# Mixing stage in another program order, weights requested two ahead, state chain on VectorE; FFN 2 with six classical tiles

## Chip, cores and metric

One core of a Trainium2 chip runs the whole layer. The metric is the device time of one execution in microseconds (us); several executions are taken and the median counts. Engines: TensorE (PE; its weight loads are PEld), VectorE (DVE), ScalarE (ACT), GpSimd (POOL) and SyncE (SP), which here issues nearly all DMAs.

## What is computed

One decoder layer on a sequence of 512 tokens with 1024 channels: a half-step SwiGLU FFN, a mixing stage in which half of the channels go through a diagonal state space model (SSM, 32 groups of 16 channels, a complex state of 64 each) and half through sliding-window attention (8 heads, 2 key/value heads, window 128, sinks, partial rotary), a second half-step FFN, and a last RMSNorm. In short:

```python
h = rms_norm(x, ffn1_norm);  x = x + 0.5 * swiglu(h, w_gate, w_up, w_down)
h = rms_norm(x, mix_norm) @ w_in          # u (512), q (512), k (128), v (128)
y_ssm = s5_mixer(u)                       # B u -> scan over time -> C -> gelu -> y * sigmoid(y @ w_glu + b)
y_att = swa_sink_attention(rope(q), rope(k), v, sinks)
x = x + concat(rms_norm(y_ssm), rms_norm(y_att)) @ w_out
h = rms_norm(x, ffn2_norm);  x = x + 0.5 * swiglu(h, w_gate2, w_up2, w_down2)
return rms_norm(x, final_norm)
```

All of it is float32, with an FFN width of 2816, that is 22 tiles of 128 (called f).

## The kernel before

**Products.** A float32 operand is split into a rounded part hi and a rest lo, and a product is three matmuls (`mm3`, L178 to L184: hi with hi, lo with hi, hi with lo). A weight is fetched by `weight` (L173): a DMA of 512 KB on SyncE's queue into `wraw` (L169), a rounding copy `whi` (ACT unless the table ENGINES names another engine, L152) and the subtraction `wlo` (VectorE by default, L171). Each of the three tiles has three buffers (pool `wp`), so a fourth request waits until the first weight's subtraction has read its `wraw`. SyncE issues in program order: a DMA that waits for its buffer holds back all behind it.

**Stages.** FFN 1 runs to about 400 us of the span, the mixing stage from there to some 591, FFN 2 to the end. The Tile scheduler orders each engine's instructions from the program order by its own simulation; pools decide which buffer is free when.

**Mixing.** The program order is written out in the string ORDER (L43); each word is a step with an index: U0 to U3 project u by a 128x512 weight each (`u_mm`, 24 matmuls of 512 columns), K0 and K1 project k and v (48 matmuls of 256 columns each), C0 to C3 project q (`tok_mm`, L1011 to L1013, tiles pt). R0 and R1 make the norm's factors; u0 to u3 scale by them and store u to a DRAM buffer `du` (L1100, L1102); l0 and l1 load half of it back as U in another layout (L1108, eight DMAs each), after the stores have landed. P0 and P1 (`ssm_state`) do the state of one half each: 32 + 32 matmuls pv with matV (L1131), four products ri (L1136 to L1139), sums zr and zi, two scans wr and wi (L1144, L1145), four products ro (L1148) and eight pieces S (L1160). L0 (`load_matT`, L966) loads matT, 2 MB, by eight DMAs of 256 KB whose rows are 512 bytes; it comes to lie in a buffer (tag "big", two of them) that one half of matV has, so it waits for P1's matmuls. Y0 and Y1 (`ssm_out`) are the matmuls with matT and U (L1175) and with matC and S (L1176). k, t, q, Q, S, E, T, V are the attention's steps; G is the SSM's gate (weight wglu), W and X the output projection (weight wout). The string ENGINES (L47) gives single instructions another engine: G is GpSimd, V VectorE, A ScalarE. By default the ro products alternate between VectorE and GpSimd, and zr and zi are GpSimd's.

**FFN 2** (`ffn2`). The first NCL tiles f are classical: 2 x 24 matmuls of 512 columns each for gate and up. The others come in pairs of tiles, and each pair is done by a seven-product (Strassen-Winograd) scheme on quarters, 2 x 7 x 4 x 3 = 168 matmuls of 256 columns (`pairs`, L513). The quarters of the normed input and their sums have to be made and split first (`quarters`, eight steps: h at L440, splits xq at L459 and L462, sums on GpSimd). PREP says how many of these steps are placed behind tile f; the rest follow one by one in the first down product. FGROUPS[2] cuts the f tiles into groups; after each group but the last `down` multiplies by the group's part of w_down, eight outputs of 128 channels (dn), and adds to x. The last group is the tail.

```python
def weight(self, src, cols, key=""):
    t = self.weight_tiles()
    self.weight_part(t, src, 0, cols, key)
    return t[1][:, :cols], t[2][:, :cols]
```

Of the kernel before, what the change touches and what calls it, by code (L numbers as in the profile page):

```python
# [29 lines left out]
HD = 64  # L30
HALF = 8
EPS = 1e-6
FGROUPS = {1: ((0, 6), (6, 12), (12, 17), (17, 22)), 2: ((0, 4), (4, 10), (10, 14), (14, 18), (18, 22))}
HEADS = [0, 1, 4, 5, 2, 3, 6, 7]
TAIL_EARLY = 0
PR_AT = (0, 0, 1)
PRB_AT = (0, 1, 3)
NCL = 4
AHEAD = 2
PREP = (1, 1, 0)  # L40
SCALED = -1.0 / 8192.0
RND = 12582912.0
ORDER = ("R0 K0 U1 K1 U0 R1 u0 U2 U3 u1 k0 l0 C0 u2 u3 P0 l1 t0 C1 P1 C2 L0 C3 q0 q3 Y0 q2 q1 Q2 Y1 Z0 Q0 Q1 "  # L43
# [3 lines left out]
ENGINES = ("higlu1=G hiout00=G loglu1=G loout00=G lowq3=G pt01=V pt11=V pt20=A pt21=V pt30=A pt31=V pt41=V "  # L47
         "pt51=V ql1=G ql3=G ro00=G ro02=G ro10=G ro11=V rope83=G s0000=G s0001=G s0010=G s0100=G s0101=G "
         "s1011=G s1111=G y001=A y011=A yh000=V yh100=V yh101=V yh111=V yl000=G yl010=G yl110=G zi0=V zr0=V "
         "zr1=V")  # L50
PIO2 = [float.fromhex("0x1.92p+0"), float.fromhex("0x1.fb4p-12"), float.fromhex("0x1.4442d18469899p-24")]


def lay_out(inp):
# [17 lines left out]
    out["wgs2"] = c(pr.transpose(0, 2, 1, 3, 4, 5).reshape((NF - NCL) // 2, 2, 2, P, 8 * P))  # L72
    f0 = FGROUPS[2][-1][0]
    out["wdt"] = c(g["ffn2_w_down"][0, f0 * P:].reshape(NF - f0, P, D))
# [58 lines left out]
class Body:  # L133
# [231 lines left out]
    def ffn(self, i, next_gain, extra):  # L365
# [7 lines left out]

        groups = FGROUPS[i]
        hooks = {(1, 1): self.first_norm, (2, 1): self.norm_bcast}
# [209 lines left out]
    def ffn2(self):  # L585
        xg, wgu, wd = self.xg, self.d["wgu2"], self.d["wd2"]
        prep, acts, pend = [], [], []
        for gi, (f0, f1) in enumerate(FGROUPS[2]):
            acts = []
            f = f0  # L590
            while f < f1:
# [22 lines left out]
                f += 1  # L614
            if gi == len(FGROUPS[2]) - 1:
                self.tail_weights(1)
# [351 lines left out]
    def mixing(self):  # L968
        nc, d = self.nc, self.d
        V, A, G, PE = nc.vector, nc.scalar, nc.gpsimd, nc.tensor  # L970
# [16 lines left out]
        self.y = [None] * 4  # L987
        self.ys = [None] * 4

        def u_mm(m):  # L990
            wh, wl = self.weight(d["wu"][m].rearrange("p k m -> p (k m)"), 1024, f"u{m}")
            pu[m] = self.ps("pu")
            for k in range(KT):
                self.mm3(pu[m], wh[:, k * P:(k + 1) * P], wl[:, k * P:(k + 1) * P], xg[k][0], xg[k][1],
                         k == 0, k == KT - 1)
# [4 lines left out]
        def tok_mm(wname, c, n, nk):  # L1000
            key = (wname, c)
            if c == 0:
                hold[wname] = [self.ps("pt") for _ in range(4)]
            wh, wl = self.weight(d[wname][c].rearrange("p k m -> p (k m)"), 1024, f"{wname}{c}")
            for kk in range(nk):
                k = c * nk + kk
                for t in range(4):
                    xs = [xg[k][i][:, t * P:(t + 1) * P] for i in range(2)]
                    wsl = slice(kk * n, (kk + 1) * n)
                    o = hold[wname][t][:, 0:n]  # L1010
                    PE.matmul(o, xs[0], wh[:, wsl], start=(k == 0), stop=False)  # L1011
                    PE.matmul(o, xs[0], wl[:, wsl], start=False, stop=False)
                    PE.matmul(o, xs[1], wh[:, wsl], start=False, stop=(k == KT - 1))  # L1013
# [49 lines left out]
        wt, po = {}, {}  # L1063

        def out_half(half, m):
            key = (half, m // 2)
            if key not in wt:
                wt[key] = self.weight(d["wout"][half, m // 2].rearrange("p k m -> p (k m)"), 1024, f"out{half}{m // 2}")
            w = wt[key]
            ps = po[half, m] = self.ps("ow")  # L1070
            for k in range(4):
                c = ((m % 2) * 4 + k) * P
                src = (self.s2, self.attn)[half][k]
                self.mm3(ps, w[0][:, c:c + P], w[1][:, c:c + P], src[0], src[1], k == 0, k == 3)
# [130 lines left out]
    def glu(self, m):  # L1205
        nc = self.nc
        if m % 2 == 0:
            self.wg = self.weight(self.d["wglu"][m // 2].rearrange("p k m -> p (k m)"), 1024, f"glu{m // 2}")
        ps = self.ps("glu")
        for k in range(4):  # L1210
            c = ((m % 2) * 4 + k) * P
            self.mm3(ps, self.wg[0][:, c:c + P], self.wg[1][:, c:c + P], self.ys[k][0], self.ys[k][1], k == 0, k == 3)
        sg = self.m2(name="sg")
        nc.scalar.activation(sg, ps, AF.Sigmoid, bias=self.b_glu[:, m:m + 1])
        y2 = self.m2(name="y2")
        self.eng(f"y2{m}").tensor_tensor(y2.rearrange("p (n s) -> p s n", s=T), self.y[m].rearrange("p (s n) -> p s n", s=T),
                                sg.rearrange("p (s n) -> p s n", s=T), op=ALU.mult)
        self.ss_ssm.add(y2, last=(m == 3))
        self.y2.append(y2)
# [294 lines left out]
```

## Time and profile before

| | us |
|---|---|
| three runs | 969.84, 961.62, 962.42 |
| median | 962.42 |
| profiled execution | 968.99 |
| its span, first to last instruction | 967.2 |
| PE busy in it | 921.6 (95%) |
| DVE busy | 649.9 (67%) |
| ACT busy | 377.2 (39%) |
| POOL busy | 348.1 (36%) |

The span is 1.8 us shorter than the execution's own time; times of single instructions are counted from the span's start. The profiled execution had a mean granted TensorE clock of 0.971. Busy shares are means over three stages: the rows below are taken from the places that the change touches.

### The profile page before, as it was taken

The numbers are of one execution on the slowest core, as the hardware profiler recorded it, in microseconds if no ns is written. First come the engines' busy times: TensorE is split into PE (matmuls) and PEld (weight loads), VectorE is DVE, ScalarE is ACT, GpSimd is POOL, SyncE is SP. The second block draws the span as 40 slices with busy tenths as digits, with TensorE's granted clock in tenths as the row PEclk, the third lists the DMA queues.
The fourth block names the chain that finished last, engine by engine and source line by source line (L and its number), as shares of the span: only waits on it lengthen the run. The fifth ranks groups of instructions, "written<-read, shape, count | busy, mean of one in ns | idle before, by whom it ended". The sixth has DMA issues, their size and how long they took to land.

```text
span 967.2 us, 13609 instructions
## 1 busy us (share of the span) xinstructions
PE 921.6 (95%) x5108; PEld 787.4 (81%) x5108; DVE 649.9 (67%) x1171; ACT 377.2 (39%) x685; POOL 348.1 (36%) x305
## 2 busy tenths in 40 slices
PE   9899899999999999999399999979999999999996
PEld 6687688888887888888388887858998898998995
DVE  7984445555644444756797478698985585886876
ACT  7132122222232223422197334434553353453553
POOL 3109411459910000405631045084550540724602
PEclk9899999999999999999798799989999999999998
DMA  6321423343323322435901032214413403405322
GB/s 234 109 83 50 119 87 121 56 134 114 93 63 118 113 70 66 145 111 151 120 1 45 1 100 74 77 43 143 139 43 111 156 23 101 140 23 170 105 65 88
DMA packets 47313, 91.95 MB, mean 95 GB/s; under 512 B 13200, under 2 KB 19088, under 8 KB 47248
## 3 DMA queue, kind: packets, MB, share of 16 engines
q1 hardware_dynamic: 46816, 90.54, 31.7%
q8 instruction: 40, 0.66, 0.3%
q10 hardware_dynamic: 432, 0.55, 0.2%
q14 instruction: 25, 0.20, 0.1%
HBM read 87.44 MB, written 3.64 MB: 94 GB/s over the span
## 4 chain that ended last, share of the span: by engine, by line
PE 77%; DVE 11%; POOL 4%; issue 3%; ACT 3%; DMA 1%; SPq 0%; DVEq 0%; POOLq 0%; ACTq 0%
PE gu L180 9%; PE gu L182 9%; PE gu L181 9%; PE dn L182 7%; PE dn L180 7%; PE dn L181 7%; PE gua L182 3%; PE gua L180 3%; PE gua L181 3%; POOL tB L632 3%; DVE wlo L534 2%; PE guc L182 2%; PE ow L180 2%; PE ow L181 2%; PE ow L182 2%
## 5 line engine op out<-in xcount | busy, mean ns | idle before, releaser
L152 ACT CAST whi<-wraw 128x1024 fp32r<-128x1024 f32 (+5 forms) x138 | 119.3, 875 | 317.1 <-PE gu L181 120.7
L171 DVE TENSOR_TENSOR wlo<-wraw,whi 128x1024 fp32r<-128x1024 f32 (+5 forms) x137 | 152.7, 1121 | 36.5 <-ACT whi L152 36.2
L182 PE MATMUL gu<-hi,wlo 128*128 128x512 f32 x416 | 164.6, 397 | 4.5 <-DVE wlo L171 4.5
L180 PE MATMUL gu<-hi,whi 128*128 128x512 f32 x416 | 167.2, 406 | 1.3 <-ACT hi L193 1.1
L181 PE MATMUL gu<-lo,whi 128*128 128x512 f32 x416 | 164.7, 397 | 0.1
L182 PE MATMUL dn<-hi,wlo 128*128 128x512 f32 (+1 forms) x336 | 130.1, 395 | 3.7 <-DVE wlo L171 3.7
L180 PE MATMUL dn<-hi,whi 128*128 128x512 f32 (+1 forms) x336 | 130.2, 396 | 2.5 <-ACT hi L201 2.4
L181 PE MATMUL dn<-lo,whi 128*128 128x512 f32 (+1 forms) x336 | 131.4, 393 | 0.0
L182 PEld LDWEIGHTS gu<-hi,wlo 128*128 128x128 f32 x416 | 78.9, 190 | 23.1 <-DVE wlo L171 4.9
L267 POOL TENSOR_TENSOR sq<-sq 128x512 f32<-128x512 f32 x24 | 35.3, 1472 | 166.2 <-ACT sq L263 163.1
L180 PEld LDWEIGHTS gu<-hi,whi 128*128 128x128 f32 x416 | 79.1, 190 | 19.7 <-ACT hi L193 1.9
L181 PEld LDWEIGHTS gu<-lo,whi 128*128 128x128 f32 x416 | 79.1, 190 | 17.7 <-DVE lo L195 1.0
L182 PEld LDWEIGHTS dn<-hi,wlo 128*128 128x128 f32 x336 | 64.2, 191 | 19.5 <-DVE wlo L171 5.0
L180 PEld LDWEIGHTS dn<-hi,whi 128*128 128x128 f32 x336 | 64.1, 191 | 18.3 <-ACT hi L201 2.9
L181 PEld LDWEIGHTS dn<-lo,whi 128*128 128x128 f32 x336 | 64.3, 191 | 13.8
L499 POOL TENSOR_TENSOR s<-s,wraw 128x512 f32<-128x512 f32 x36 | 59.5, 1653 | 39.4 <-DMA wraw<-wgs 25.7
L499 POOL TENSOR_TENSOR s<-wb 128x512 f32<-128x512 f32 x18 | 26.6, 1477 | 116.1 <-DMA wb<-wgs 108.9
L534 DVE TENSOR_TENSOR wlo<-s,whi 128x512 fp32r<-128x512 f32 x72 | 58.0, 849 | 9.0 <-ACT whi L533 9.0
L410 DVE SCALAR_TENSOR_TENSOR x<-dn,x 128x512 f32<-128x512 f32 x32 | 21.7, 687 | 47.9 <-PE dn L182 47.9
L533 ACT CAST whi<-s 128x512 fp32r<-128x512 f32 x72 | 41.4, 618 | 31.8 <-PE gua L181 9.4
L343 DVE TENSOR_TENSOR u<-gu,R 128x512 f32<-128x512 f32 x26 | 17.8, 686 | 49.7 <-PE gu L182 49.0
L426 DVE SCALAR_TENSOR_TENSOR x<-dn,x 128x512 f32<-128x512 f32 x32 | 21.7, 687 | 35.6 <-PE dn L182 35.6
(376 smaller groups left out, 2164.6 us busy)
## 6 DMA issues: line engine op xcount, KB each, us to landing
wraw<-wgu SPq DMA_DIRECT2D x50, 512.0 KB, 3.5
wraw<-wd SPq DMA_DIRECT2D x24, 384.0 KB, 3.2
wb<-wgs SPq DMA_DIRECT2D x36, 256.0 KB, 4.6
wraw<-wgs SPq DMA_DIRECT2D x18, 512.0 KB, 3.8
wraw<-wd SPq DMA_DIRECT2D x24, 256.0 KB, 2.7
wraw<-wd SPq DMA_DIRECT2D x16, 320.0 KB, 2.9
wraw<-wout SPq DMA_DIRECT2D x8, 512.0 KB, 3.5
x<-xT SPq DMA_DIRECT2D x8, 256.0 KB, 5.0
```

Source lines behind the costliest of these rows:

```text
L152: (e.copy if e is self.nc.scalar else e.tensor_copy)(out, x)
L171: self.eng("lo" + key).tensor_tensor(lo, raw, hi.bitcast(F32), op=ALU.subtract)
L180: mm(out, wh, xh, start=start, stop=False, **kw)
L181: mm(out, wh, xl, start=False, stop=False, **kw)
L182: mm(out, wl, xh, start=False, stop=stop, **kw)
L267: b.nc.gpsimd.tensor_tensor(self.acc, self.acc, sq, op=ALU.add)
L410: nc.vector.scalar_tensor_tensor(self.x[m], ps, 0.5, self.x[m], op0=ALU.mult, op1=ALU.add)
L426: self.nc.vector.scalar_tensor_tensor(self.x[m], ps, 0.5, self.x[m], op0=ALU.mult, op1=ALU.add)
L499: add = lambda o, x, y: nc.gpsimd.tensor_tensor(o, x, y, op=ALU.add)
L533: self.chained("A", lambda: A.copy(hi[:, c], w))
L534: self.chained("V", lambda: V.tensor_tensor(lo[:, c], w, hi[:, c].bitcast(F32), op=ALU.subtract))
L632: (eng or V).tensor_tensor(out, a, b, op=op)
```

## The change

**Mixing.** ORDER has U0, U1 and U2 ahead of K0 and K1, the first load of U (l0) and P0 earlier, and the first and second half of K before and after P0. ENGINES puts all ro products and zr and zi of both halves on VectorE and names no engine for S, whose default is VectorE. `fetch` takes the place of `weight` for the stage's 16 weights: it lists them in the order in which ORDER first needs them, and a step that takes one also requests those up to WAHEAD - 1 further in the list.

**FFN 2.** NCL goes from 4 to 6, so one pair less is left; the groups are three of six tiles and the tail; PREP has five entries instead of three.

```diff
-FGROUPS = {1: ((0, 6), (6, 12), (12, 17), (17, 22)), 2: ((0, 4), (4, 10), (10, 14), (14, 18), (18, 22))}
+FGROUPS = {1: ((0, 6), (6, 12), (12, 17), (17, 22)), 2: ((0, 6), (6, 12), (12, 18), (18, 22))}
-NCL = 4
+NCL = 6
 AHEAD = 2
-PREP = (1, 1, 0)
+WAHEAD = 2
+PREP = (0, 1, 1, 1, 0)
-ORDER = ("R0 K0 U1 K1 U0 R1 u0 U2 U3 u1 k0 l0 C0 u2 u3 P0 l1 t0 C1 P1 C2 L0 C3 q0 q3 Y0 q2 q1 Q2 Y1 Z0 Q0 Q1 "
+ORDER = ("R0 U0 U1 R1 u0 u1 l0 U2 K0 P0 U3 u2 u3 K1 k0 l1 C0 P1 t0 C1 L0 C2 C3 q0 q3 Y0 q2 q1 Q2 Y1 Z0 Q0 Q1 "
...
+        names = {"U": lambda m: (f"u{m}", d["wu"][m]), "K": lambda c: (f"wkv{c}", d["wkv"][c]),
+                 "C": lambda c: (f"wq{c}", d["wq"][c]), "G": lambda m: (f"glu{m // 2}", d["wglu"][m // 2]),
+                 "W": lambda m: (f"out0{m // 2}", d["wout"][0, m // 2]),
+                 "X": lambda m: (f"out1{m // 2}", d["wout"][1, m // 2])}
+        srcs = dict(names[step[0]](int(step[1])) for step in ORDER.split() if step[0] in names)
+        need, got = list(srcs), {}
+
+        def fetch(key):
+            at = list(srcs).index(key)
+            while need and list(srcs).index(need[0]) < at + WAHEAD:
+                n = need.pop(0)
+                got[n] = self.weight(srcs[n].rearrange("p k m -> p (k m)"), 1024, n)
+            return got.pop(key)
+
+        self.fetch = fetch
+
         def u_mm(m):
-            wh, wl = self.weight(d["wu"][m].rearrange("p k m -> p (k m)"), 1024, f"u{m}")
+            wh, wl = fetch(f"u{m}")
```

The other calls of `weight` in the stage (`tok_mm`, `out_half`, `glu`) become `fetch` in the same way.

**The order before and after.** On SyncE, from the q weights (wq) to matT, before:

```order
L169 DMA wraw<-wq 128x1024 x4
L1102 DMA du<-u 128x512 x2
L1108 DMA U<-du 16x16x64 x8
L1102 DMA du<-u 128x512
L169 DMA wraw<-wglu 128x1024
L1102 DMA du<-u 128x512
L169 DMA wraw<-wglu 128x1024
L1108 DMA U<-du 16x16x64 x8
L169 DMA wraw<-wout 128x1024 x2
L966 DMA matT<-dz 16x32x128 x8
```

and after:

```order
L169 DMA wraw<-wq 128x1024 x2
L1118 DMA du<-u 128x512 x2
L169 DMA wraw<-wq 128x1024
L1124 DMA U<-du 16x16x64 x8
L169 DMA wraw<-wq 128x1024
L1118 DMA du<-u 128x512 x2
L1124 DMA U<-du 16x16x64 x8
L169 DMA wraw<-wglu 128x1024 x2
L169 DMA wraw<-wout 128x1024 x2
L966 DMA matT<-dz 16x32x128 x8
```

Both stores of u2 and u3 and the second load of U now stand ahead of both wglu requests; matT still follows two wout. On VectorE between the chain of P0 and that of P1 (names with a number are ri and ro of one half), before, from P0's last sum on:

```order
L1142 TENSOR_TENSOR zi<-ri_3773,ri_3774 128x512
L1144 SCALAR_TENSOR_TENSOR wr<-rho,zr 128x512
L1145 SCALAR_TENSOR_TENSOR wi<-rho,zi 128x512
L1037 TENSOR_TENSOR kL<-tk,kH 64x512
L1160 TENSOR_TENSOR S<-ro_3787,ro_3788 64x4x63
L171 TENSOR_TENSOR wlo<-wraw,whi 128x1024
L1136 TENSOR_TENSOR ri_3891<-pv,ec 128x512
L1037 TENSOR_TENSOR kL<-tk,kH 64x512
L1137 TENSOR_TENSOR ri_3892<-pv,es 128x512
L1138 TENSOR_TENSOR ri_3893<-pv,ec 128x512
L1139 TENSOR_TENSOR ri_3894<-pv,es 128x512
L1160 TENSOR_TENSOR S<-ro_3789,ro_3790 64x4x63 x2
```

and after, from the same place:

```order
L1158 TENSOR_TENSOR zi<-ri_3618,ri_3619 128x512
L1160 SCALAR_TENSOR_TENSOR wr<-rho,zr 128x512
L1161 SCALAR_TENSOR_TENSOR wi<-rho,zi 128x512
L1164 TENSOR_TENSOR ro_3632<-wr,ec 128x512
L1164 TENSOR_TENSOR ro_3633<-wi,es 128x512
L1164 TENSOR_TENSOR ro_3634<-wr,es 128x512
L1164 TENSOR_TENSOR ro_3635<-wi,ec 128x512
L1116 TENSOR_TENSOR u<-pu,R 128x512 x2
L1176 TENSOR_TENSOR S<-ro_3632,ro_3633 64x4x63 x4
L171 TENSOR_TENSOR wlo<-wraw,whi 128x1024
L1176 TENSOR_TENSOR S<-ro_3634,ro_3635 64x4x63 x4
```

The ro products of P0 are rows of VectorE now and stand ahead of the last two u, and all eight pieces S of P0 follow these; ten rows further down P1's first ri comes, right behind the wlo of the first wglu. On VectorE in FFN 2 around the splits xq of the quarter inputs (g, u, a, lo are the activation's steps), before:

```order
L339 TENSOR_TENSOR g<-gu,R 128x512
L459 TENSOR_TENSOR xq<-h,xq 128x256
L171 TENSOR_TENSOR wlo<-wraw,whi 128x512
L459 TENSOR_TENSOR xq<-h,xq 128x256
L343 TENSOR_TENSOR u<-gu,R 128x512
L459 TENSOR_TENSOR xq<-h,xq 128x256 x6
L345 TENSOR_TENSOR a<-s,u 128x512
L459 TENSOR_TENSOR xq<-h,xq 128x256 x4
L171 TENSOR_TENSOR wlo<-wraw,whi 128x512
L203 TENSOR_TENSOR lo<-a,hi 128x512
L462 SCALAR_TENSOR_TENSOR xq<-qe,xq 128x512
L339 TENSOR_TENSOR g<-gu,R 128x512
```

and after:

```order
L339 TENSOR_TENSOR g<-gu,R 128x512
L459 TENSOR_TENSOR xq<-h,xq 128x256 x3
L171 TENSOR_TENSOR wlo<-wraw,whi 128x1024
L459 TENSOR_TENSOR xq<-h,xq 128x256 x9
L343 TENSOR_TENSOR u<-gu,R 128x512
L171 TENSOR_TENSOR wlo<-wraw,whi 128x1024
L345 TENSOR_TENSOR a<-s,u 128x512
L203 TENSOR_TENSOR lo<-a,hi 128x512
L171 TENSOR_TENSOR wlo<-wraw,whi 128x1024
L339 TENSOR_TENSOR g<-gu,R 128x512
L462 SCALAR_TENSOR_TENSOR xq<-qe,xq 128x512
L462 SCALAR_TENSOR_TENSOR xr<-q_5631,xr 128x512
```

The 512-column wlo of before are down weights; the 1024-column ones of after are weights of gate and up, so the twelve splits have moved from the end of the last classical tile and the first down product to the middle of the classical tiles.

## Rows read from the trace of the kernel before

**Rows 1.** What TensorE waited for: us in total, times, longest us
```profile
PE py L1175 <- DVE rb L1119: 14.7, 1, 14.7
```
**Rows 2.** TensorE's timeline, FFN 2: start us, us, instruction, [idle before <- releaser]
```profile
638.72 0.39 PE L180 MATMUL dn<-hi,whi 128*128 128x512 f32 x1
638.95 0.40 PE L181 MATMUL dn<-lo,whi 128*128 128x512 f32 x1
...
642.71 0.73 PE L180 MATMUL dn<-hi,whi 128*128 128x512 f32 x2 [2.43 <-ACT hi L201]
...
646.66 0.80 PE L182 MATMUL dn<-hi,wlo 128*128 128x512 f32 x1 [2.99 <-DVE wlo L171]
...
669.91 0.28 PE L180 MATMUL gua<-xq,whi 128*128 128x256 f32 x1
...
698.09 0.39 PE L182 MATMUL guc<-xq,wlo 128*128 128x256 f32 x1 [1.58 <-DVE wlo L534]
```
**Rows 3.** SyncE's timeline, mixing: start us, us of issuing, DMA
```profile
442.08 5.08 SPq L1108 DMA_DIRECT2D U<-du  x8
...
455.58 10.64 SPq L966 DMA_DIRECT2D matT<-dz  x8
```
**Rows 4.** Line L966, from 464 to 465 us: issue, and issue to landing
```profile
L966 SPq DMA_DIRECT2D matT<-dz x1: 2176/2176/2176, 464.0 to 464.0; - x1
...
DMA to landing us min/median/max: 13.3/13.3/13.3
```
**Rows 5.** TensorE's timeline, mixing
```profile
400.62 0.28 PE L1011 MATMUL pt<-whi,hi 128*128 128x256 f32 x1
...
449.66 2.08 PE L1131 MATMUL pv<-U,matV 128*64 128x64 f32 x64
...
477.76 0.70 PE L1175 MATMUL py<-matT,U 128*64 128x128 f32 x4 [14.65 <-DVE rb L1119]
```
**Rows 6.** Stretches: us, busy (x) of PE, PEld, DVE, ACT, POOL; PEclk, DMA share, GB/s
```profile
456.00:458.00 2.00, 2.00 (x10) 1.65 (x9) 1.97 (x4) 0.00 (x0) 1.87 (x3) 1.00 0.87 285
466.00:474.00 8.00, 0.00 (x0) 0.00 (x0) 7.88 (x10) 0.29 (x1) 7.92 (x11) 0.55 1.22 113
525.00:545.00 20.00, 20.00 (x90) 19.22 (x90) 7.04 (x16) 7.71 (x24) 0.00 (x0) 0.50 0.00 1
643.00:651.00 8.00, 5.01 (x13) 3.70 (x13) 7.90 (x10) 2.18 (x5) 5.34 (x6) 0.58 0.13 35
670.00:690.00 20.00, 20.00 (x169) 20.00 (x168) 16.59 (x22) 9.71 (x21) 13.27 (x9) 1.00 0.33 107
```
**Rows 7.** VectorE's timeline, mixing, and one row of ScalarE's
```profile
426.35 2.21 DVE L1100 TENSOR_TENSOR u<-pu,R 128x512 f32<-128x512 f32 x2
...
431.45 1.23 DVE L171 TENSOR_TENSOR wlo<-wraw,whi 128x1024 fp32r<-128x1024 f32 x1
...
442.75 0.69 DVE L1136 TENSOR_TENSOR ri<-pv,ec 128x512 f32<-128x512 f32 x1 [4.38 <-PE pv L1131]
...
447.82 1.20 DVE L1145 TENSOR_TENSOR_SCAN wi<-rho,zi 128x512 f32<-128x512 f32 x1
...
449.77 1.04 ACT L152 CAST whi<-wraw 128x1024 fp32r<-128x1024 f32 x1 [4.35 <-PE pt L1013]
```
**Rows 8.** DMAs issued from 395 to 500 us: count, KB each, median us to landing
```profile
du<-u SPq DMA_DIRECT2D x4, 256.0 KB, 3.3
...
wraw<-wglu SPq DMA_DIRECT2D x2, 512.0 KB, 5.0
```
**Rows 9.** DMA traffic from 466 to 474 us, and a weight issued there
```profile
DMA packets 1818, 0.90 MB, mean 113 GB/s; under 512 B 58, under 2 KB 1818, under 8 KB 1818
...
wraw<-wout SPq DMA_DIRECT2D x1, 512.0 KB, 8.3
```
**Rows 10.** Line L1160 (the S pieces): ns min/median/max of one
```profile
L1160 DVE TENSOR_TENSOR S<-ro,ro x9: 577/1470/2548, 451.4 to 474.5; 64x252 f32<-64x252 f32 x9
```
**Rows 11.** Line L459 (split of the quarter inputs): ns min/median/max of one
```profile
L459 DVE TENSOR_TENSOR xq<-h,xq x12: 408/950/961, 632.6 to 644.5; 128x256 fp32r<-128x256 f32 x12
```

More of the change, by code (lines that the diff above doesn't have):

```diff
@@ L47 @@
 ENGINES = ("higlu1=G hiout00=G loglu1=G loout00=G lowq3=G pt01=V pt11=V pt20=A pt21=V pt30=A pt31=V pt41=V "
-         "pt51=V ql1=G ql3=G ro00=G ro02=G ro10=G ro11=V rope83=G s0000=G s0001=G s0010=G s0100=G s0101=G "
-         "s1011=G s1111=G y001=A y011=A yh000=V yh100=V yh101=V yh111=V yl000=G yl010=G yl110=G zi0=V zr0=V "
-         "zr1=V")
+           "pt51=V ql1=G ql3=G y001=A y011=A yh000=V yh100=V yh101=V yh111=V yl000=G yl010=G yl110=G zi0=V zi1=V "
+           "zr0=V zr1=V ro00=V ro01=V ro02=V ro03=V ro10=V ro11=V ro12=V ro13=V")
 PIO2 = [float.fromhex("0x1.92p+0"), float.fromhex("0x1.fb4p-12"), float.fromhex("0x1.4442d18469899p-24")]
@@ L1003, in tok_mm @@
                 hold[wname] = [self.ps("pt") for _ in range(4)]
-            wh, wl = self.weight(d[wname][c].rearrange("p k m -> p (k m)"), 1024, f"{wname}{c}")
+            wh, wl = fetch(f"{wname}{c}")
             for kk in range(nk):
@@ L1067, in out_half @@
             if key not in wt:
-                wt[key] = self.weight(d["wout"][half, m // 2].rearrange("p k m -> p (k m)"), 1024, f"out{half}{m // 2}")
+                wt[key] = fetch(f"out{half}{m // 2}")
             w = wt[key]
@@ L1207, in glu @@
         if m % 2 == 0:
-            self.wg = self.weight(self.d["wglu"][m // 2].rearrange("p k m -> p (k m)"), 1024, f"glu{m // 2}")
+            self.wg = self.fetch(f"glu{m // 2}")
         ps = self.ps("glu")
```

## Prediction

> **What bounds the kernel now.** First I read the list of what TensorE waited for, because a change of program order can only pay where TensorE stands still. The longest entry is 14.7 us in front of the first matmul of Y0 (py, L1175) [rows 1]. Everything else in the layer is small beside it; around the changed part of FFN 2 the waits are 2.43, 2.99 and 1.58 us [rows 2]. So two places are priced: the wait before Y0, and the first down product of FFN 2.
>
> **The wait before Y0.** The list names a rope product on VectorE (rb, L1119) as the releaser [rows 1]. I doubt that. Y0's first matmul reads matT and U. The matT load is eight DMAs, requested by SyncE from 455.58 on [rows 3]; the last is issued at 464.0 and lands 13.3 us later, at 477.3 [rows 4]. TensorE starts at 477.76 [rows 5]. A rope product is no input of Y0; it only happens to end beside it. From 466 to 474 the load moves 113 GB/s, while a weight at 456 to 458 moved 285 GB/s [rows 6]. So the wait ends when matT is there, and matT is there some 22 us after its first request: what counts is when SyncE reaches that request. In the program it stands behind both loads of U, both wglu and two wout weights, and behind P1's matmuls, whose matV holds the buffer; these run from 449.66 to 451.7 [rows 5], so in before it was the queue and not P1 that set 455.58.
>
> **When matT is requested after the change.** TensorE enters the stage at 400.62 [rows 5] and now does 72 matmuls of 512 columns (U0, U1, U2) first. A 512-column matmul follows the last by 0.23 us (638.72 to 638.95) [rows 2]; 169 of 256 columns fill 20 us, 0.118 each [rows 6]. That gives 400.6 + 72 x 0.23 = 417.2, and I allow 1.3 for the norm's small matmuls between them: 418.5. The first two u need R, the norm's broadcast, which follows U1 in program order; I put their end at 420.4 (an estimate: it depends on that small chain), where before, behind 96 matmuls of K (11.3 us), they ended at 426.35 + 2.21 = 428.56 [rows 7]. Storing u and loading U takes some 0.9 to issue, 3.3 to land [rows 8] and 5.1 for the eight loads [rows 3]: U is there at about 429.7. Meanwhile TensorE does 90 of K's matmuls, 10.6 us, to 429.1, so P0's pv, 2.1 us [rows 5], can run from 429.7 to 431.8 and VectorE's chain begins at 431.0. From its first product to the end of the second scan it took 442.75 to 449.02 before, 6.3 us [rows 7]: 437.3. Here the first change of engines counts. The four ro products are now all on VectorE, at 0.65 each (six products and a scan of 1.2 fill the 5.07 us from 442.75 to 447.82 and the second scan's start), 2.6 us: 439.9. Behind them, in VectorE's order, stand u2 and u3, 2.2 us: 442.1. Everything that SyncE does next is late by that. Issue, store and landing give 445.7, U's loads 5.1: 450.8. Before, that second load ran from 442.08 to 447.16 [rows 3]. So some 8 us won at the front of the stage have become 3.6 lost here.
>
> Next the queue issues wglu (0.4) and two wout. The second wout needs a weight slot, which wglu's split has to leave: its landing takes 5.0 [rows 8], ACT's rounding 1.04, VectorE's subtraction 1.23 [rows 7]; with 0.2 between them that is 458.3, and the issue takes 0.3. matT is requested at about 458.6 instead of 455.58: **+3.0 us**. P1's chain on VectorE now stands behind that same subtraction, but it feeds Y1, not Y0; from 458.3 on its 6.3 + 2.6 us and eight S pieces at 0.7 end near 473, before matT. The ends for this term: P1's matmuls cannot end before some 454.2, which holds matV's buffer, so at best -1.4; with the slowest landing of a weight in this stretch, 8.3 [rows 9], it is +6.3. I take +3.0 as it uses wglu's own row. What TensorE did while waiting is unchanged in sum, so this shift passes to the end undiminished. The ro, zi and S pieces taken from GpSimd cost TensorE nothing as long as matT is last: S on VectorE took 577 to 2548 ns beside GpSimd [rows 10], and pieces alone should be at the low end. Without that cover they would matter for Y1 alone.
>
> **The first down product of FFN 2.** Before, it runs from 638.72 to 669.91, 31.2 us for 96 matmuls [rows 2]; at 0.23 they need 22.3, so 8.9 are lost: 2.43 and 2.99 in waits, the rest in slow matmuls, with a granted clock of 0.58 in 643 to 651 [rows 6]. The cause is VectorE, busy 7.90 of these 8 us [rows 6] with the splits of the quarter inputs, which take 950 ns where the fastest took 408 [rows 11], as GpSimd works beside them. The new PREP starts the quarters one f later and leaves six classical f tiles to run beside them, with 11.0 us each (48 x 0.23) and only two weight splits. By VectorE's order twelve splits of the quarters now stand around the weight splits of f4 and f5. Adding them up (four h at 1.7, an estimate from xq's 0.95 for half the columns, twelve xq at 0.8 to 0.95, the weights' 1.23, from 631 on) the split for f5's gate comes about 2.5 us after TensorE wants it. The down itself should run free. So -8.9 + 2.5 = **-6.4**. The ends: nothing left of the stall, -8.9; the stall merely moved, 0.
>
> [...]
>
> **More classical work.** Tiles f4 and f5 cost 96 matmuls of 512 columns, 22.3 us, in place of a Strassen pair of 168 of 256 columns, 168 x 0.118 = 19.9: **+2.4**. That is certain to a few tenths. Groups change from pairs of 3, 2, 2, 2 to 3, 3, 2. The first group of three stalled 1.58 us [rows 2] and less elsewhere; a second such group I put at **+0.5** (0 to 2.2). One down product fewer starts: 8 accumulations less on VectorE, hidden.
>
> **Sum.** +3.0 - 6.4 + 2.4 + 0.5 = -0.5. The profiled execution took 968.99, 6.6 above the median 962.42; on its own basis the changed kernel comes to 968.5, on the median's to 961.9. I predict 961.9. Ends of the terms together: -1.4 - 8.9 + 2.2 = -8.1 and +6.3 + 0 + 2.6 + 2.2 = +11.1, which no execution will have all at once; the likeliest case alone reaches from 955 to 968.
>
> **Rivals.**
> R1, the wait before Y0 mostly goes. If matT moved at the 285 GB/s of a weight [rows 6], its 2.1 MB would take 7.4 us and be there at 458.6 + 7.4 = 466, against TensorE's arrival at 477.76 - 14.65 = 463.1 [rows 5]; of 14.65 about 11.7 would go: 962.4 - 11.7 - 3.5 = 947.2. It needs matT to be slowed by something that the change removes, such as GpSimd's work or the wout weights; a list that names VectorE speaks for it. Against it: nothing of matT's transfer is changed, and its packets stay as small as 0.90 MB / 1818 = 495 bytes [rows 9]. [...]
>
> R2, slower through SyncE's queue: the place is wglu, now asked for behind the second loads of U. Each microsecond by which it lands late delays wout, matT and Y0 one for one. With 8.3 instead of 5.0 [rows 8, 9] matT slips 6.3, and the sum is -0.5 + 3.3 = +2.8: 965.2. It decides from the point where matT's request passes 459.1, since the other terms give back 3.5. For it: the sign turns on half a microsecond. Against: in before wglu landed in 5.0.
>
> R3, the clock. In the profiled execution TensorE ran at a granted 0.50 from 525 to 545, with 20 us busy and no wait [rows 6]; on the assumption that the runs near 969.8 have this stretch and those near 962 do not, a median run of the changed kernel may fall on either side: 961.9 + 6.6 = 968.5. For it: one of three runs of before did.
>
> R4, the change does what it says for FFN 2 alone, with matT's request unmoved (+0): 958.9; within the forecast's range.
>
> **How the numbers follow.** The forecast with R4 gets 0.52, R1 0.11, R2 0.17, R3 0.20. About 1%, 9.6 us, is what a measurement of this kernel can tell from no change: faster is below 952.8, slower above 972.0. R1 is faster (0.11), and of the rest 0.04, where both FFN 2 ends come out well. Slower needs R2 and R3 together or the upper ends of several terms: 0.09. The rest, 0.76, is the same. For eight in ten I leave out R1's lower half and the top of R2 with R3: 950 to 971.
>
> **What would show it.** Right: in the changed profile matT's first request between 457 and 461 and Y0's start some 22 us behind it, still TensorE's longest wait; u2 and u3 at about 442 on VectorE; no wait over 1 us inside the first down of FFN 2 and its length near 33.5 us for 144 matmuls; a wait of 1 to 4 us at f5. Wrong: Y0 starting before 472, or a matT request before 454; a first down that still has a stretch below full clock; or a new wait before Y1 or the transposes of q, which would mean that VectorE, now carrying the whole state chain, had become the bound.

## The result, and the profile after

| | before | after |
|---|---|---|
| median of six runs | 965.99 us | 954.70 us |
| lowest, highest | 961.62, 969.84 | 953.79, 956.96 |
| profiled execution | 968.99 | 955.14 |

The ratio is 0.9896 with a 95% interval of 0.986 to 0.9932: 1.0% faster, with the bound of 1% inside the interval. The time lies 7 us below the predicted 961.9, within the range of 950 to 971 and above the 952.8 below which the prediction would have called it faster. The six runs of before are of two kinds, 961.6 to 963.6 and 968.4 to 969.8; the six of after are of one. Why that is so is part of the answer.

What TensorE waited for, after (us in total, times, longest us):

```profile
PE py L1191 <- DMA wraw<-wout: 15.4, 1, 15.4
PE gu L182 <- DVE wlo L171: 5.1, 2, 4.8
...
PE sc L1272 <- DVE qT L1077: 2.9, 2, 1.6
PE pt L1321 <- ACT pr L1300: 1.7, 1, 1.7
```

The wait before Y0 is still there and as long as in [rows 1]. Its releaser is now named as the DMA of a wout weight, which Y0 reads as little as it reads the rope product named before; matT's last DMA, issued at 466.5, takes 12.2 us to land, that is until 478.8, and Y0 starts at 479.08:

```profile
L966 SPq DMA_DIRECT2D matT<-dz x2: 2279/2656/3032, 463.5 to 466.5; - x2
...
DMA to landing us min/median/max: 12.2/13.4/14.5
```

The waits in the first down product of FFN 2 [rows 2] have left the list. The sc row is new: two waits before the scores, for the transposed q that VectorE finishes. Every profile with the change's order has them (1.3 to 1.4 and 1.6 us), engines_before with the old engines too, and none with the order of before. TensorE's timeline at the borders of the stages, after (start us, us, instruction):

```profile
400.50 0.40 PE L180 MATMUL pu<-hi,whi 128*128 128x512 f32 x1
...
479.08 0.70 PE L1191 MATMUL py<-matT,U 128*64 128x128 f32 x4 [15.42 <-DMA wraw<-wout]
...
586.41 0.40 PE L180 MATMUL gu<-hi,whi 128*128 128x512 f32 x1
...
646.02 0.50 PE L182 MATMUL gu<-hi,wlo 128*128 128x512 f32 x1 [0.33 <-DVE wlo L171]
...
656.81 0.39 PE L180 MATMUL dn<-hi,whi 128*128 128x512 f32 x1
...
690.62 0.28 PE L180 MATMUL gua<-xq,whi 128*128 128x256 f32 x1
...
751.31 0.39 PE L180 MATMUL dn<-hi,whi 128*128 128x512 f32 x1
...
784.78 0.28 PE L180 MATMUL gua<-xq,whi 128*128 128x256 f32 x1
...
845.47 0.39 PE L180 MATMUL dn<-hi,whi 128*128 128x512 f32 x1
...
945.07 0.40 PE L1491 MATMUL po<-whi,lo 128*128 128x512 f32 x1
```

and the rows of before at the borders that [rows 2] and [rows 5] lack:

```profile
591.22 0.40 PE L180 MATMUL gu<-hi,whi 128*128 128x512 f32 x1
...
733.35 0.39 PE L180 MATMUL dn<-hi,whi 128*128 128x512 f32 x1
...
959.26 0.40 PE L1475 MATMUL po<-whi,lo 128*128 128x512 f32 x1
```

From these: the mixing stage (first matmul of the stage to first of FFN 2) takes 185.9 us after against 190.6 before, FFN 2 (to TensorE's last matmul) 359.1 against 368.4. The two differences, 4.7 and 9.4, are the profiled 13.8 to within 0.3. They are of different make. Granted clock and busy time, after (columns as in [rows 6]):

```profile
525.00:545.00 20.00, 19.29 (x153) 17.99 (x152) 15.23 (x42) 13.86 (x36) 2.64 (x2) 1.00 0.09 28
643.00:651.00 8.00, 7.67 (x33) 5.92 (x32) 6.69 (x10) 2.92 (x5) 0.51 (x2) 1.00 0.24 58
656.81:690.62 33.81, 33.74 (x145) 27.07 (x144) 21.82 (x28) 10.62 (x16) 12.17 (x8) 1.00 0.49 149
```

Both stretches that ran at 0.50 and 0.58 before [rows 6] run at 1.00. The second lay in the first down product before and lies ahead of it now; the first down product itself, 656.81 to 690.62, is at 1.00 as well, so that FFN 2's stall is gone and not moved. The first stretch had no wait in it before. Up to Y0 nothing was won: Y0 starts 78.6 us behind the stage's first matmul (479.08 - 400.50), before 77.1 (477.76 - 400.62) [rows 5]. SyncE's timeline, after:

```profile
440.95 1.38 SPq L1118 DMA_DIRECT2D du<-u  x2
444.07 4.42 SPq L1124 DMA_DIRECT2D U<-du  x8
448.60 2.26 SPq L169 DMA_DIRECT2D wraw<-wglu  x2
450.95 4.43 SPq L169 DMA_DIRECT2D wraw<-wout  x2
455.47 13.35 SPq L966 DMA_DIRECT2D matT<-dz  x8
```

matT is requested 55.0 us into the stage, as in before (455.58 - 400.62 = 55.0) [rows 3, 5]. On VectorE in FFN 2, after:

```profile
626.09 6.91 DVE L440 SCALAR_TENSOR_TENSOR h<-x,gains,R 128x512 f32<-128x512 f32 x4
...
637.32 6.92 DVE L459 TENSOR_TENSOR xq<-h,xq 128x256 fp32r<-128x256 f32 x9
...
644.76 1.21 DVE L171 TENSOR_TENSOR wlo<-wraw,whi 128x1024 fp32r<-128x1024 f32 x1
```

The weight split behind the nine xq begins at 644.76, and TensorE waits 0.33 us for it, where I had put 2.5.

### The profile page after: what moved, and what is told of

Its sections match the earlier page's. It is cut to its first block, busy times and chain, and to the rows that moved or that the text cites. A ratio compares the mean times of both kernels' runs of the same rounds, so it can differ in the third digit from the quotient of the medians.

```text
span 953.1 us, 13351 instructions
## 1 busy us (share of the span) xinstructions
PE 912.1 (96%) x5036; PEld 776.7 (81%) x5036; DVE 638.5 (67%) x1160; ACT 369.4 (39%) x660; POOL 317.3 (33%) x279
## 4 chain that ended last, share of the span: by engine, by line
PE 76%; DVE 11%; POOL 4%; DMA 3%; ACT 2%; SPq 2%; issue 2%; ACTq 0%; DVEq 0%
PE gu L180 8%; PE gu L182 8%; PE gu L181 8%; PE dn L180 7%; PE dn L181 7%; PE dn L182 7%; PE gua L182 3%; PE gua L181 3%; PE gua L180 3%; POOL tB L632 3%; PE guc L181 2%; PE guc L182 2%; PE guc L180 2%; PE ow L180 2%; PE ow L182 2%
## 5 line engine op out<-in xcount | busy, mean ns | idle before, releaser
L152 ACT CAST whi<-wraw 128x1024 fp32r<-128x1024 f32 (+4 forms) x134 | 122.6, 921 | 319.0 <-PE gu L181 109.9
L171 DVE TENSOR_TENSOR wlo<-wraw,whi 128x1024 fp32r<-128x1024 f32 (+4 forms) x133 | 159.3, 1202 | 38.3 <-ACT whi L152 37.3
L182 PE MATMUL gu<-hi,wlo 128*128 128x512 f32 x448 | 177.3, 397 | 5.1 <-DVE wlo L171 5.1
L180 PE MATMUL gu<-hi,whi 128*128 128x512 f32 x448 | 180.0, 405 | 1.0 <-ACT hi L193 0.7
L181 PE MATMUL gu<-lo,whi 128*128 128x512 f32 x448 | 177.6, 397 | 0.1
L182 PEld LDWEIGHTS gu<-hi,wlo 128*128 128x128 f32 x448 | 84.9, 190 | 25.5 <-DVE wlo L171 6.0
L180 PEld LDWEIGHTS gu<-hi,whi 128*128 128x128 f32 x448 | 85.1, 190 | 21.0 <-ACT whi L152 1.7
L181 PEld LDWEIGHTS gu<-lo,whi 128*128 128x128 f32 x448 | 85.0, 190 | 19.3 <-DVE lo L195 1.3
L181 PEld LDWEIGHTS dn<-lo,whi 128*128 128x128 f32 x336 | 63.8, 190 | 13.8
L499 POOL TENSOR_TENSOR s<-s,wraw 128x512 f32<-128x512 f32 x32 | 50.4, 1574 | 33.5 <-DMA wraw<-wgs 32.5
L410 DVE SCALAR_TENSOR_TENSOR x<-dn,x 128x512 f32<-128x512 f32 x32 | 21.6, 687 | 46.9 <-PE dn L182 46.9
L533 ACT CAST whi<-s 128x512 fp32r<-128x512 f32 x64 | 36.5, 618 | 29.4 <-PE gua L181 10.4
L426 DVE SCALAR_TENSOR_TENSOR x<-dn,x 128x512 f32<-128x512 f32 x24 | 16.5, 690 | 44.2 <-PE dn L182 44.1
```

The source lines that it names most:

```text
L152: (e.copy if e is self.nc.scalar else e.tensor_copy)(out, x)
L171: self.eng("lo" + key).tensor_tensor(lo, raw, hi.bitcast(F32), op=ALU.subtract)
L180: mm(out, wh, xh, start=start, stop=False, **kw)
L181: mm(out, wh, xl, start=False, stop=False, **kw)
L182: mm(out, wl, xh, start=False, stop=stop, **kw)
L410: nc.vector.scalar_tensor_tensor(self.x[m], ps, 0.5, self.x[m], op0=ALU.mult, op1=ALU.add)
```

## The experiments

Each was read by its stages, since FFN 1, which no experiment but own35 changes, ends between 399.7 and 406.3 in these profiles: a difference of total times below that says nothing alone. The stage times of all profiles, from TensorE's timelines, in us:

| profile | matT requested | Y0 | mixing stage | Y0 to FFN 2 | FFN 2 |
|---|---|---|---|---|---|
| before | 55.0 | 77.1 | 190.6 | 113.5 | 368.4 |
| before_a | 54.9 | 77.8 | 183.7 | 105.9 | 368.1 |
| after | 55.0 | 78.6 | 185.9 | 107.3 | 359.1 |
| after_again | 54.4 | 75.8 | 182.3 | 106.5 | 359.0 |
| mix_only | 56.0 | 78.8 | 186.2 | 107.3 | 368.8 |
| ffn2_only | 54.9 | 78.1 | 193.7 | 115.6 | 359.1 |
| old_prep | 54.6 | 77.6 | 184.9 | 107.3 | 358.7 |
| ncl4_prep | 54.2 | 77.2 | 183.4 | 106.2 | 369.0 |
| engines_before | 51.9 | 74.3 | 182.8 | 108.5 | 358.8 |
| rows16 | 55.1 | 76.6 | 183.5 | 106.9 | 358.5 |
| spread | 54.6 | 72.0 | 179.3 | 107.3 | 358.5 |
| spread_again | 55.0 | 73.0 | 180.3 | 107.3 | 358.6 |
| own35 | (in FFN 1) | 62.8 | 179.9 | 117.1 | 359.0 |
| spread_v | 54.7 | 76.8 | 194.1 | 117.2 | 358.6 |

Times in the second and third column count from the stage's first matmul.

FFN 1 is of two kinds. In eight of the profiles, own35 left out, it ends between 399.7 and 401.5; in before_a, after_again, engines_before, old_prep and spread_v between 404.7 and 406.3. In these five, and in no other, one split of a down weight on VectorE takes 10.9 to 11.0 us, where no other weight split on VectorE takes over 2.4 in any profile. It ends 0.8 us behind a chain of 0.6 us products on GpSimd (L632) that runs beside it, and TensorE waits 10 us for it. From before_a:

```profile
94.09 10.94 DVE L171 TENSOR_TENSOR wlo<-wraw,whi 128x768 fp32r<-128x768 f32 x1
...
102.79 1.42 POOL L632 TENSOR_TENSOR aB<-tB 128x256 f32<-128x256 f32 x2
```

```profile
PE dn L182 <- DVE wlo L171: 13.0, 2, 10.0
```

So a total can be 5 us higher for a reason that lies in no edit.

**The two halves of the change.** mix_only is the changed kernel with FFN 2 as before (FGROUPS[2] of before, and):

```diff
-NCL = 6
+NCL = 4
-PREP = (0, 1, 1, 1, 0)
+PREP = (1, 1, 0)
```

> The change in the mixing stage alone (program order, engines, fetch), FFN 2 as before. Theory: this part moves matT's first request by less than 1 us, so Y0 starts at 479 +- 1 instead of 477.8; the half-clock stretch of 6 to 7 us near 525 to 545 does not appear with this order, in any execution; FFN 2 is as before with its first down product near 31 us. Time 964.5 +- 1.5 in all rounds, that is as the lower level of before's runs (961.6 to 963.6) plus 1 to 2. Rival A, the new order saves time by itself: 957 to 960. Rival B, the term as I predicted it (+3.0): 965.5 to 967.

Median 963.65 of 12 runs, ratio to before 0.9994 (0.9961 to 1.0027). Ten of twelve runs lie between 960.5 and 964.4, two above (967.3 and 974.5). matT's request moved by 1.0, Y0 by 1.7. Rival A falls; the theory holds but for "in all rounds", and for matT's request, which moved by as much as the theory set for its limit. What the two high runs had is not known; their granted clocks are 0.975 and 0.968, those of the other ten 0.978 to 0.981.

ffn2_only is the kernel before with the change of FFN 2 (FGROUPS[2] of the change, and):

```diff
-NCL = 4
+NCL = 6
-PREP = (1, 1, 0)
+PREP = (0, 1, 1, 1, 0)
```

> The change in FFN 2 alone (six classical tiles, groups of six, PREP with five entries), mixing as before. Theory: FFN 2 is 9.4 us shorter, the first down product has no wait over 1 us, and the first group of three pairs takes 60.7 us instead of 63.4; the times lie at two levels as before's do, 953 and 959.5, since the mixing stage with its half-clock stretch is unchanged. Rival, the predicted sum for FFN 2 (-3.5, with a wait of 2.5 us at the fifth tile and a second stalling group): 959 and 965.5.

Median 958.69, ratio 0.9921 (0.9884 to 0.9959). FFN 2 takes 359.1, the 9.4 us less in full, and the runs lie at two levels, six between 952.1 and 955.9 and five between 961.5 and 962.9 (one at 968.2); the upper level is 2.5 us above the expected 959.5. The granted clock parts the two: 0.978 to 0.984 in the lower six, 0.972 to 0.974 in the upper five. The profiled execution is an upper one (962.02) and has the slow stretch, at 527 to 547.5. The rival, my sum for FFN 2, falls. So the whole lasting gain is FFN 2's, and the mixing change brings something only against the upper level.

**What the two levels are.** before_a is the kernel before, unchanged, profiled in another execution: do its two levels (961.6 to 963.6 and 968.4 to 969.8 in the result) differ by the stretch that ran at a granted 0.50 in [rows 6]?

> The kernel before, once more, for a profile of another execution. [...] If this execution is on the lower level its mixing stage takes 184 us from TensorE's first matmul there to its first of FFN 2, and the granted clock of 525 to 545 is above 0.9; if on the upper, 190.6 and 0.5. Rival: the levels differ elsewhere, the stretch is there at either.

967.37, but its mixing stage took 183.7 and the stretch of 525 to 545 ran at full clock:

```profile
525.00:545.00 20.00, 18.72 (x158) 17.76 (x156) 15.60 (x36) 14.51 (x36) 4.43 (x3) 1.00 0.10 35
```

In [rows 6] the same program had 90 matmuls in that stretch at 0.50, here 158 at 1.00; from Y0 to FFN 2 the difference is 113.5 - 105.9 = 7.6 us. So the stretch at a granted 0.50 is a matter of the execution and not of the program alone. The expectation is only half met, though: by its time this execution belongs to the upper level, and yet it has no such stretch; it is high since its FFN 1 ended 5.7 later (406.3). A time near 968 can thus come from the stretch or from FFN 1, and the time alone does not tell which; the granted clock, 0.971 in before's profiled run and 0.975 here, helps. With it the mixing change is seen at equal clock: 183.7 before, in one profile; 182.3 to 186.2 in the five profiles with the change's order, engines and fetch (after, after_again, mix_only, old_prep, ncl4_prep), 184.5 in the mean. It costs about 1 us or nothing; one profile of before cannot say more. None of these five has the slow stretch, and no run of the changed kernel in either series (six and six, 951.1 to 957.0) lies at a second level: their granted clocks are 0.980 to 0.986.

**PREP or classical tiles.** old_prep:

```diff
-PREP = (0, 1, 1, 1, 0)
+PREP = (1, 1, 0, 0, 0)
```

> The changed kernel with before's PREP (first steps of the quarters behind tiles 1 and 2), six classical tiles kept. Theory: the stall in the first down product of before came from too few classical tiles beside the splits, not from where PREP puts them; with six tiles the splits end before the down product in either case: time as the changed kernel, 954.7 +- 1. Rival, PREP is what takes the stall away: 3 to 6 us slower, 958 to 961, with waits over 1 us at tiles 3 and 4 or in the down product.

Median 960.97 of four runs (952.8 to 963.5), ratio 0.9885 (0.9799 to 0.997). By its times the rival would have it (958 to 961), by its stages the theory: FFN 2 takes 358.7 and has no wait over 0.6, so PREP's new entries bring nothing. Of the profiled execution's 958.87, 5 us are FFN 1's later end; why two of the four runs took 963 no profile shows. The splits start at the same place as with four tiles (the first h 34.9 us into FFN 2, as in mix_only), and end 52.1 us in, 17.7 ahead of the first down product.

ncl4_prep, with FGROUPS[2] of before:

```diff
-NCL = 6
+NCL = 4
-PREP = (0, 1, 1, 1, 0)
+PREP = (1, 1, 1)
```

> The changed kernel with four classical tiles and before's groups, and PREP (1, 1, 1), that is one step of the quarters more ahead of the first down product than in before. Theory: VectorE's splits still meet the down product's weights, so the waits of 2.4 and 3.0 us and the slow stretch behind them stay: 963 to 965, as the run mix_only. Rival, the earlier step is enough: the stall goes, and without the 2.2 us of added classical work the time is 953 to 955.

Median 967.17, ratio 0.9961 (0.9925 to 0.9997), above the expected 963 to 965: two of ten runs took 961.7 and 961.9, the other eight 966.2 to 970.7. The profile is of a low one, so what the eight had is not shown. FFN 2 takes 369.0, and TensorE's timeline shows the waits of before again:

```profile
634.90 0.73 PE L180 MATMUL dn<-hi,whi 128*128 128x512 f32 x2 [2.42 <-ACT hi L201]
638.86 0.79 PE L182 MATMUL dn<-hi,wlo 128*128 128x512 f32 x1 [3.00 <-DVE wlo L171]
```

The added entry of PREP left the splits where they were (the first h 35.0 us into FFN 2, before 35.0), so the rival's earlier step was not in fact tried. The first down product starts 47.5 us into FFN 2 here, while the splits last until 54.3; with six tiles, in old_prep, it starts at 69.7, behind them. So it is the number of classical tiles (with the groups that go with it) that takes the waits away: TensorE's 11 us in each give VectorE the time for the splits.

**What Y0 waits for, and what that wait is worth.** own35, with L0 moved to the head of ORDER:

```diff
-        self.m2p = ctx.enter_context(tc.tile_pool(name="m2p", bufs=43))
+        self.m2p = ctx.enter_context(tc.tile_pool(name="m2p", bufs=35))
-        self.matT = self.big("matT").rearrange("p (g x) -> p g x", g=NG)
+        self.matT = self.cp.tile([P, 4096], F32, name="matT").rearrange("p (g x) -> p g x", g=NG)
```

> The changed kernel with a buffer of its own for matT, loaded at the start of the mixing stage; to make room the pool m2 has 35 buffers instead of 43. Theory, Y0 waits for matT alone: Y0 starts within 3 us of TensorE's arrival near 463.7, and the time falls by 8 to 15 us to 940 to 947, less if the smaller pool or the state chain of P1 makes Y1 late. Rival, VectorE's chain holds Y0 as the list for the kernel before says: Y0 not before 475, time 953 to 957.

Median 962.23, ratio 0.9981 (0.9954 to 1.0007). matT was requested in FFN 1, at 192 to 200. Y0 started 62.8 us into the stage, behind other matmuls without a wait: matT was what held it, and the rope product of [rows 1] was not. But the mixing stage became only 6.0 us shorter than after's, and 2.4 shorter than after_again's. What TensorE waited for, own35:

```profile
PE tq L1067 <- DVE rb L1135: 9.7, 1, 9.7
PE dn L180 <- ACT whi L152: 5.9, 1, 5.9
```

Of 15.4 us, 9.7 come back at the transposes of q, whose rotary stands behind P1's chain on VectorE. The total is high because FFN 1 ended about 11 us later, and what the trace shows behind it is the moved load, not the smaller pool: two down weights requested behind matT's eight DMAs, at 203.2 and 205.5, took 13.3 and 11.9 us to land, and ScalarE's rounding waited for them, and TensorE for that (the second row above):

```profile
216.50 0.83 ACT L152 CAST whi<-wraw 128x768 fp32r<-128x768 f32 x1 [8.34 <-DMA wraw<-wd]
```

rows16, in which dz is laid out anew:

```diff
-        dz = S.dp.tile([SC, NG, 15, SC], F32, name="dz")
+        dz = S.dp.tile([SC, 15, NG, SC], F32, name="dz")
...
-            self.nc.sync.dma_start(self.matT[j * SC:(j + 1) * SC], zv[:, :, j * SC:(j + T) * SC])
+            self.nc.sync.dma_start(t[j * SC:(j + 1) * SC], zv[:, j * 512:(j + T) * 512])
+        self.matT = t.rearrange("p (b g e) -> p g b e", b=T, g=NG)
```

> The changed kernel with the DRAM buffer dz laid out so that each partition of matT is read as one run of 16 KB instead of 32 runs of 512 bytes; the Y matmuls then read matT in blocks of 16. Theory, matT's arrival ends the wait before Y0 and its rate of some 113 GB/s comes from the short runs: the rate rises above 200 GB/s, Y0 starts at 466 to 470 and the time falls to 943 to 947. Rival, the rate has another cause or VectorE's chain holds Y0: Y0 at 477 or later, 953 to 957; reading in blocks could add 1 to 2 us to Y.

Median 951.92, ratio 0.9879 (0.9841 to 0.9917). The data packets grew from 512 bytes (0.90 MB in the 1760 of [rows 9] that are not under 512) to 16 KB (1.41 MB in 86), and the rate did not, with 117 GB/s against 113. The mean of 495 bytes in the prediction counts 58 small packets that add next to nothing to these bytes, as do the 86 here. DMA traffic of rows16 from 462 to 474:

```profile
DMA packets 172, 1.41 MB, mean 117 GB/s; under 512 B 86, under 2 KB 86, under 8 KB 86
```

The theory of short runs falls. What was left in common is that each of the eight DMAs writes 16 of the 128 partitions, from one DRAM buffer. spread, against rows16:

```diff
-        for j in range(T):
-            self.nc.sync.dma_start(t[j * SC:(j + 1) * SC], zv[:, j * 512:(j + T) * 512])
+        for x in range(0, 4096, 1024):
+            src = self.dz.rearrange("c b g e -> c (b g e)")[:, x:x + 1024]
+            src = bass.AP(tensor=src.tensor, offset=src.offset, ap=[[512, T]] + [list(s) for s in src.ap])
+            self.nc.sync.dma_start(t[:, x:x + 1024], src)
```

> The kernel of the run rows16, with matT loaded by four DMAs that each write all 128 partitions (512 KB, runs of 4 KB) in place of eight DMAs that each write 16 partitions. Theory: matT's slow rate of 113 GB/s comes from a DMA writing only 16 partitions at a time, so the rate rises to a weight's (above 200 GB/s), matT is there 10 us after its request, near 466, and Y0 starts at 466 to 468 instead of 479; of these 12 us about half are lost again at the transposes of q, where VectorE's chain is late (9.7 us in the run own35): the time falls by 5 to 8 us to 947 to 950. Rival, the rate belongs to the source in DRAM: Y0 at 477, time 952.

> The run spread again, in more rounds. Theory: its mixing stage of 179.3 us, 6.6 shorter than the changed kernel's, is lasting: 947 to 949, that is 6 to 7 us under after_again. Rival: as after_again within 2 us, the first profile having been a lucky one.

spread: median 952.24 of four (947.3 to 955.2), ratio 0.9819 (0.9732 to 0.9907). spread_again: 951.03 of six, ratio 0.9852 (0.9805 to 0.9899). While matT moves alone, between the landing of the last weight ahead of it and the request of the next, in spread, spread_again and spread_v, a run told further down (columns as in [rows 6]):

```profile
457.10:461.60 4.50, 4.50 (x21) 3.61 (x20) 4.50 (x3) 0.00 (x0) 4.50 (x4) 1.00 0.49 178
```

```profile
459.40:462.80 3.40, 3.40 (x16) 2.73 (x15) 3.40 (x2) 0.00 (x0) 3.40 (x4) 1.00 0.50 157
```

```profile
464.40:467.90 3.50, 3.50 (x17) 2.85 (x16) 3.50 (x5) 1.23 (x3) 0.00 (x0) 1.00 0.53 125
```

TensorE's row at Y0 in spread_again:

```profile
474.53 0.70 PE L1193 MATMUL py<-matT,U 128*64 128x128 f32 x4 [10.27 <-DMA matT<-dz]
```

In spread and spread_again the rate rises to 178 and 157 GB/s, not above 200 as expected, and the DMA engines are busy for half of that time only, where the old load kept them busy throughout (a share of 0.99 in rows16 and 1.22 in [rows 6]). From matT's request to Y0 it takes 17.4 and 18.0 us (spread, spread_again) instead of 21.4 to 23.6, not the 12 or so expected; the next wout, requested 7.4 and 6.3 us behind matT and before that has landed, is under way beside it for the rest. But the third execution with the spread load, spread_v, has 125 GB/s and 22.2 us to Y0, as slow as the old load, which moved 132 GB/s from 462 to 474 in engines_before. So that the 16 written partitions held the old load is my estimate from spread and spread_again alone, and not shown; what held the new one, the source in DRAM for one, stays open. The mixing stage is 179.3 and 180.3, 2 to 7 us under the profiles with the change's loads; in the times, against after_again on the same chip, it is 1.2 us, which the intervals do not part and which is the rival's "within 2 us". So two stages show a gain, the times do not.

> The changed kernel again, for comparison with spread_again on one chip: 954 to 957 where nothing is disturbed, mixing stage 185 to 187 us, FFN 2 359.1 us to TensorE's last matmul.

after_again: median 952.22 of six, ratio 0.9857 (0.9814 to 0.99): the result again, 2 us below the 954 to 957 expected, with a mixing stage of 182.3 where 185 to 187 was expected.

spread_v, with four splits taken from GpSimd:

```diff
-ENGINES = ("higlu1=G hiout00=G loglu1=G loout00=G lowq3=G pt01=V pt11=V pt20=A pt21=V pt30=A pt31=V pt41=V "
+ENGINES = ("lowq3=G pt01=V pt11=V pt20=A pt21=V pt30=A pt31=V pt41=V "
```

> The run spread, with the splits of the second wglu and the first wout on ScalarE and VectorE instead of GpSimd, so that GpSimd does nothing beside P1's chain. Theory: after matT the next to end is VectorE's chain of P1 and the rotary of q, some scans and products of which took 2 to 3.4 us instead of 1.2 and 0.7 beside GpSimd; alone they are 6 us shorter, against 2.4 us of added splits, so the wait at the transposes of q shrinks by 2 to 4 us and the time is 944 to 948. Rival, the added splits eat the gain: as spread, +- 1.

Median 954.89 of four runs that lie between 949.6 and 968.6. Its one profile has a stretch at a granted 0.50 (531 to 551, 95 matmuls, TensorE busy for all 20 us), late in the attention part as in before, and matT came late in it (76.8, the third row above), so the theory on the transposes of q is not tested: inconclusive. It does show that the change's order by itself does not exclude that stretch.

**The engines.** engines_before is the changed kernel with the whole string ENGINES of before.

> The changed kernel with before's table of engines (half of ro, one zi and seven S pieces back on GpSimd, and S, ro and zi free for either), the new order kept. By the prediction's working u2 and u3 leave VectorE 2.6 us earlier, and wglu, wout and matT are requested up to 2.6 us earlier: Y0 76 to 77.5 us behind TensorE's first matmul of the stage instead of 78.6. Rival: GpSimd's work slows VectorE's beside it and matT is held by P1's matmuls in either, Y0 at 78 to 80; then the engines make no difference to the end.

956.58 in its one run. matT is requested 51.9 us into the stage instead of 55.0 and Y0 starts at 74.3, earlier than the theory's 76 to 77.5; by FFN 2 it is back at 182.8, among the profiles with the changed engines. VectorE's u2 and u3 start 36.5 us into the stage instead of 39.3, as predicted from the four products in front of them; one wglu is also requested ahead of the loads of U here. So the state chain on VectorE does cost matT its 3 us, most of it by these products, and in this one execution no gain that could be told from the spread of the stage is left at its end, as the rival says.

## Why the prediction was right or wrong

The time fell within the range, but that is owed to the range's width and not to the sum: -0.5 was forecast and about -11 measured between the medians, and three of the four terms erred to the same side.

**The wait before Y0 stays: right, and for the reason given.** own35 shows that matT is what it waits for. The chance of 0.11 for R1 was fair; its price of 11.7 us was too high: own35, spread and spread_again are 5.6 to 6.6 us shorter in mixing than after and 2.0 to 3.0 shorter than after_again, the same kernel, so only 2 to 7 us reach FFN 2. For the same reason a shift of matT does not pass to the end undiminished, as I had it. My point against R1, small packets, was wrong: rows16 has large ones, of 16 KB, and 117 GB/s, no more than the 109 to 132 of the small ones (after and engines_before, 462 to 474).

**matT's request, +3.0: mechanism right, size wrong.** It came out at 0.0. The front of the chain came as worked out: P0's products began at 431.2, the last two u were stored from 440.95. The rest was sized too long by single rows of before: the store landed 2.0 us after its issue where I took 3.3, U's loads took 4.4 and not 5.1 (they ended 2.3 us sooner than worked out), and wglu landed in 4.0 where I took 5.0, so that wout's second request came 3 us sooner in all. With that, P1's matmuls, which I had as the lower end, ended at 454.7, 0.8 ahead of matT's request. R2, which lived on the same rows, had no place.

**The first down product, -6.4: the step that failed is the left-over of 2.5 us.** It measured 0.33, so this term is -8.6. VectorE's chain was not sized too long: seven of the nine splits in the 6.92 us took 0.95 to 0.96 each and two 0.41, and from the first h (626.09) to the end of the gate's split (644.76 + 1.21) it took 19.9 us with three other instructions between, where the prediction's rows add up to 17.6 to 19.4. What came later is TensorE. It reached f5's gate 58.7 us into FFN 2:

```profile
645.06 0.40 PE L180 MATMUL gu<-hi,whi 128*128 128x512 f32 x1
```

Five tiles at the prediction's 11.0 us make 55; the small products of the norm and a wait of 0.7 us in the first tiles are not in them. The prediction does not write down when TensorE wants that split, so that this is where the 2.5 came from is likely and not shown. That the stall would leave the down product was right, and old_prep against mix_only shows why: six classical tiles, not PREP, which I had named with them.

**Classical work, +2.4: right.** From FFN 2's first matmul to the first down 70.4 us after (586.41 to 656.81) against 47.5 before, 22.9 more; a pair saves about 20.2 (three pairs in 60.69), and 0.33 is the wait just named.

**The second group of three pairs, +0.5: wrong in sign.** I took the 1.58 us wait [rows 2] for a property of such a group. In after both groups take 60.69 us (690.62 to 751.31, 784.78 to 845.47); the one of before took 63.44 (669.91 to 733.35). The three other profiles with the stall (before_a, mix_only, ncl4_prep) have waits of 1.6 us or of 0.8 twice there, and the profiles with six tiles none over 0.6, so the wait looks like the tail of the first down's stall, from which VectorE comes late; that is argued, as the number of tiles differs too. This term is -2.75, and with some 0.6 in later groups FFN 2 sums to -8.6 + 2.4 - 2.75 - 0.6 = -9.5; measured is -9.4.

**The clock, R3: the assumption was right, its place in the argument wrong.** before and before_a show that the stretch comes and goes with the execution and is worth 7 us, and ffn2_only has two levels by it. But I let the changed kernel have it as often as before. Of before's six runs one has it by its profile and two more may have it by their times, though before_a warns that FFN 1 can look the same; none of the changed kernel's twelve has it by time or clock. In the series of mix_only 13 of 29 runs of before have a granted clock of 0.973 or less. If half of before's runs have it, that adds about half of 7 us to the difference of the medians: -9.4 for FFN 2, about +1 for mixing, -3 for the clock, against -11.3 measured. The last two are fitted afterwards, and FFN 1's two kinds are not in them. Why this order meets it more rarely stays open: the waits ahead of it differ (0.20 and 1.27 us at 519 to 523 before, 0.71 at 527 after), but before_a has 1.28 there as well and kept its clock.

## What to carry to other kernels

A stall that follows another can be its echo: price it with the first before taking it for a rate of the later loop. Before an edit is credited or blamed, cut every profile into stages, for here FFN 1 moved by 5 us and mixing by 7 without any edit, each almost as much as the edit was worth. A wait that ends a chain of requests is worth only the distance to the next chain: of 15 us before Y0, 2 to 7 reached the end of the stage. And read a rate where the load in question moves alone.

## What the runs showed of the hardware that was not expected

Eight DMAs that each write 16 partitions moved 113 GB/s in packets of 512 bytes (108 to 132 over the profiles) and 117 GB/s in packets of 16 KB, so the packet size was not the limit here; four that write all 128 partitions moved the same data at 178 and 157 GB/s in two executions and at 125 in a third, with a busy share of the DMA engines of 0.49 to 0.53. One and the same program ran 20 us of its attention part at a granted 0.50, with TensorE busy throughout, in one execution and at 1.00 in another, worth 7 us. And in five of thirteen profiles of an unchanged FFN 1 one subtraction on VectorE lasted 10.9 to 11.0 us and ended 0.8 us behind a chain of products on GpSimd beside it, and FFN 1 ended about 5 us later.
